# Memory attention of a decoder layer on Trainium2: which weight rests are made by adding transfers, and where the query weight sums are loaded

## The chip, the core and the metric

The kernel runs on one core of a Trainium2 chip. The core has a matrix engine (PE, with PEld for its weight loads), a vector engine (DVE), a scalar engine (ACT), GpSimd (POOL) and SyncE (SP). Each works through its own instructions in order and waits for the others by semaphores. Transfers between DRAM and the on-chip memory are issued by an engine and carried out by 16 DMA engines, which the queues of all issuers share; here SP issues the plain loads and POOL the loads that add onto what is already in the tile ("adding transfers").

The metric is the time of one execution in device microseconds (us), as the median of several runs.

## The reference

One decoder layer over 512 tokens of width 1024 with a memory of 256 rows: a half-step of a gated feed-forward network, token mixing, cross-attention to the memory, a second half-step and a final norm. The change touches the cross-attention alone:

```python
def memory_xattn(h, m, w_xq, w_xkv, w_xo):
    B, S, _ = h.shape
    q = (h @ w_xq).reshape(B, S, XATTN_HEADS, XATTN_HEAD_DIM) * XATTN_HEAD_DIM ** -0.5
    k, v = jnp.split(m @ w_xkv, 2, axis=-1)
    k = k.reshape(B, -1, XATTN_HEADS, XATTN_HEAD_DIM)
    v = v.reshape(B, -1, XATTN_HEADS, XATTN_HEAD_DIM)
    p = jax.nn.softmax(jnp.einsum('bshd,bmhd->bhsm', q, k).astype(jnp.float32), axis=-1)
    o = jnp.einsum('bhsm,bmhd->bshd', p.astype(v.dtype), v)
    return o.reshape(B, S, D_MODEL) @ w_xo
...
        x = x + memory_xattn(rms_norm(x, norm_xattn[l]), rms_norm(mem, norm_mem[l]), w_xq[l], w_xkv[l], w_xo[l])
```

B is 1, S is 512, D_MODEL is 1024, and there are 4 heads of 256.

## The kernel before

Every matrix product is made from operands that are split in two: a head `h` in the type fp32r, and a rest `l`, which is the float32 value minus the head. A product then takes three matmuls: h with h, h with l, l with h. There are two ways to the rest of a weight:

- `split` (L113): ACT copies the raw weight into `h`, DVE subtracts `h` from the raw weight.
- `added` (L1478): ACT copies the raw weight into `h`, ACT writes the negated copy into `l`, and POOL issues a transfer that reads the same weight from DRAM once more and adds it onto `l`.

The **memory stage** (from L1443) computes keys and values of the memory. Its 16 weights `kv`, numbered i = 0 to 15, are 128 x 1024 each (512 KB): i = 0 to 7 are the key weights `in_w_xk`, each with 24 matmuls of 256 columns, and i = 8 to 15 are the value weights `in_w_xv`, each with 12 matmuls of 512 columns. Value weights 8 to 11 add up into the bank `ps_s`, 12 to 15 into `ps_t`. All 16 pass through a ring of three raw tiles (`wr`); `fetch` (L1467) loads the next one on SP's queue. `cut` (L1484) makes head and rest of a weight: into two pairs of half tiles, named `w`, for the weights in `LOOSE`; else into a whole pair, named `wh`/`wl` for i = 5 and 6 and `xqh`/`xql` for the others. `share` (L1473) takes `added` for the weights in `SHARED` and `split` for the rest. Each cut is followed by the fetch of the weight three further on.

From the loop over i on, the order of the instructions on every engine is the order in which the code is written (`ordered`). One turn of the loop: cut one weight ahead (two in the first turn), the matmuls of weight i, the keys of weight i - 1 taken out of their bank, the extras of that turn, and one or two pieces of `work`, which scale the input x and split its sums for the query products (the tiles `K`, `nh`, `nl`). After the last cut the raw tiles serve the query weights of the heads (`load_r`, L1541).

The **query products** of a head (`heads`, L1703) follow a scheme of seven products instead of eight, so they need sums of the query weight `in_w_xq`. The tile `xs` (called `s` in the code, 128 x 1536) holds them: two blocks are loaded by `load_q` (L1529, SP) and completed by an adding transfer in `add_q` (L1535, POOL); the third is a sum of the second with a part of the raw tile `r1`. For head 0 the loop also splits these: `w1` is the pair made from `r1` (its left half is read by the first of the products), `w2` the pair made from `xs`. `part` is `split` for one half of 512 columns. The second product reads the right half of `w2` (the first loaded block), the third the left half (the sum), the fourth the right half of `w1`; the second loaded block is split inside `heads` for a later product.

The extras that the loop places are (NKV is 16):

```python
                if i in (0, 2):
                    load_q(i // 2)
                elif i in (3, 5):
                    add_q(i // 5)
```

Of the kernel before, what the change touches and what calls it, by code (L numbers as in the profile page):

```python
# [71 lines left out]
def hybrid_layer(ctx: ExitStack, tc: tile.TileContext, a: dict):  # L72
# [16 lines left out]
    @contextmanager  # L89
    def ordered():  # L90
        Engine.pinned = True
        yield
        Engine.pinned = False
# [19 lines left out]
    def split(h, l, src):  # L113
        A.activation(h, src, AF.Copy)  # L114
        V.tensor_sub(l, src, f32(h))  # L115

    def wpair():
        return (g.tile([P, 1024], F32R, tag="wh", name="wh", bufs=2),
                g.tile([P, 1024], F32R, tag="wl", name="wl", bufs=2))
# [811 lines left out]
    with tc.tile_pool(name="mix", bufs=1, reuse_waits="tile") as mp:  # L931
# [121 lines left out]
        for c in range(4):  # L1053
            h, l = wload(a["vcat"][:, c * 2 * VC:(c + 1) * 2 * VC], 2 * VC)
            for kk in range(2):
                k = 2 * c + kk
                w = slice(kk * VC, (kk + 1) * VC)
# [385 lines left out]
    with tc.tile_pool(name="xa", bufs=1, reuse_waits="tile") as xp:  # L1443
# [11 lines left out]
        def part(hl, src, j):  # L1455
            split(*hl, src[:, j * 512:j * 512 + 512])
# [4 lines left out]
        kv = [a["w_xk"][m] for m in range(KT)] + [a["w_xv"][f, c] for f in range(2) for c in range(4)]  # L1461
        NKV = len(kv)
        raws, cuts = [], []
        SHARED = (7, 9, 11, 13)
        LOOSE = (0, 1, 2, 7, 8, 9, 12, 13, 14)

        def fetch():  # L1467
# [5 lines left out]
        def share(i, h, l, c):  # L1473
            if i not in SHARED:
                return split(h, l, raws[i][:, c])
            added(h, l, raws[i][:, c], kv[i][:, c])

        def added(h, l, raw, src):  # L1478

            A.activation(h, raw, AF.Copy)  # L1480
            A.activation(l, raw, AF.Copy, scale=-1.0)
            G.dma_start(l, src, accum_op=ALU.add)

        def cut():  # L1484
            i = len(cuts)
            if i in LOOSE:
                cuts.append([[big(F32R, "w0") for _ in range(2)] for _ in range(2)])
                for j in range(2):
                    share(i, cuts[i][0][j], cuts[i][1][j], slice(j * S, j * S + S))
            else:  # L1490
                cuts.append(wpair() if i in (5, 6) else qpair())
                share(i, *cuts[i], slice(0, 1024))
            fetch()
# [6 lines left out]
        def memory(i):  # L1500
            h, l = cuts[i]
            if i < KT:
                pk[i] = bank("d")
                for k in range(KT):
                    for z, (w, m) in enumerate(((h, gh[k]), (h, gl[k]), (l, gh[k]))):
                        w = w[k // 4][:, k % 4 * P:][:, :P] if i in LOOSE else w[:, k * P:(k + 1) * P]
                        T.matmul(pk[i][:, :MEM], w, m, start=k + z == 0, stop=k == KT - 1 and z == 2)
                return
            c = i % 4
            pk[i] = [bank("st"[i // 4 - 2]) for _ in range(MT)] if c == 0 else pk[i - 1]  # L1510
            for kk in range(2):
                k = 2 * c + kk
                w = slice(kk * 512, kk * 512 + 512)
                for t in range(MT):
                    tk = slice(t * P, (t + 1) * P)
                    for z, (m, ww) in enumerate(((gh, h), (gh, l), (gl, h))):
                        T.matmul(pk[i][t], m[k][:, tk], ww[kk] if i in LOOSE else ww[:, w], start=k + z == 0,
                                 stop=k == KT - 1 and z == 2)

        def evacuate(i):  # L1520
            if i < KT:
                split(kh[i], kl[i], pk[i][:, :MEM])
            elif i % 4 == 3:
                for t in range(MT):
                    split(vh[t][i // 4 - 2], vl[t][i // 4 - 2], pk[i][t])
# [3 lines left out]
        def load_q(hd):  # L1529
            w1 = a["w_xq"][2 * hd + 1]  # L1530
            xw[hd]["s"] = xp.tile([P, 1536], F32, tag="S", name="xs3", bufs=2)
            t = xw[hd]["s"][:, 512:].rearrange("p (j c) -> p j c", j=2)
            SY.dma_start(t, bass.AP(w1.tensor, w1.offset, [[1024, P], [0, 2], [1, 512]]))

        def add_q(hd):  # L1535
            w0 = a["w_xq"][2 * hd]
            t = xw[hd]["s"][:, 512:].rearrange("p (j c) -> p j c", j=2)
            G.dma_start(t, bass.AP(w0.tensor, w0.offset, [[1024, P], [P * 1024 + 512, 2], [1, 512]]),
                        accum_op=ALU.add)

        def load_r(hd):  # L1541
            xw[hd]["r1"] = raw_tile()
            SY.dma_start(xw[hd]["r1"], a["w_xq"][2 * hd])

        def load_r2(hd):
            d = xw[hd]
            d["r2"] = xp.tile([P, 1024], F32, tag="R2", name="r2", bufs=1)
            SY.dma_start(d["r2"][:, :512], a["w_xq"][2 * hd + 1][:, 512:])
# [55 lines left out]
        with ordered():  # L1604
            for i in range(NKV):
                for _ in range(1 if i else 2):
                    if len(cuts) < NKV:
                        cut()
                    elif len(cuts) == NKV and "r1" not in xw[0]:
                        load_r(0)  # L1610
                        load_r2(0)
                        load_r(1)
                        load_r(2)
                memory(i)
                if i == 0:
                    st = n3.sums()
                    n3.r = n3.rstd(st, NT)
                elif i == 1:
                    n3.spread()
                if i:  # L1620
                    evacuate(i - 1)
                if i in (0, 2):
                    load_q(i // 2)
                elif i in (3, 5):
                    add_q(i // 5)
                if i == NKV - 4:
                    d = xw[0]
                    d["w2"], w = wpair(), wpair()
                    d["w1"] = [[t[:, c:c + 512] for t in w] for c in (0, 512)]
                    added(*w, d["r1"], a["w_xq"][0])  # L1630
                    part([t[:, 512:] for t in d["w2"]], d["s"], 1)
                elif i == NKV - 3:
                    V.tensor_add(d["s"][:, :512], d["s"][:, 1024:], d["r1"][:, :512])
                    part([t[:, :512] for t in d["w2"]], d["s"], 0)
                for _ in range(0 if i < 2 else 1 if i < 9 else 2):
                    if work:
                        work.pop(0)()
            while work:
                work.pop(0)()
            evacuate(NKV - 1)  # L1640
# [274 lines left out]
```

## Time and profile before

| | |
|---|---|
| time, median of 3 runs | 1245.64 us (1244.54 to 1246.74) |
| time of the profiled execution | 1245.68 us |
| its span, first to last instruction | 1243.9 us |
| mean granted TensorE clock | 0.997 |
| DMA packets, bytes | 64944, 181.38 MB |
| queue q1 (plain loads) | 132.70 MB, 32.4% of the 16 engines' span |
| queue q0 (POOL's transfers) | 46.63 MB, 18.3% |
| chain that ended last, by engine | PE 92%, DVE 3%, DMA 2% |

The time of an execution is a little longer than the span between its first and last instruction (here 1.8 us). The chain that ended last is followed back from the last instruction, at each step to what released it. Of the page's 40 slices, each 31.1 us long, the memory stage fills most of the 24th and the 25th, which read (busy shares in tenths, and GB/s):

| | slice 24 | slice 25 |
|---|---|---|
| PE busy | 9 | 7 |
| DMA busy | 7 | 7 |
| GB/s | 230 | 202 |

### The profile page before, as it was taken

The numbers are of one execution on the slowest core, as the hardware profiler recorded it, in microseconds if no ns is written. First come the engines' busy times: TensorE is split into PE (matmuls) and PEld (weight loads), VectorE is DVE, ScalarE is ACT, GpSimd is POOL, SyncE is SP. The second block draws the span as 40 slices with busy tenths as digits, with TensorE's granted clock in tenths as the row PEclk, the third lists the DMA queues.
The fourth block names the chain that finished last, engine by engine and source line by source line (L and its number), as shares of the span: only waits on it lengthen the run. The fifth ranks groups of instructions, "written<-read, shape, count | busy, mean of one in ns | idle before, by whom it ended". The sixth has DMA issues, their size and how long they took to land.

```text
span 1243.9 us, 19322 instructions
## 1 busy us (share of the span) xinstructions
PE 1226.9 (99%) x7113; PEld 1070.2 (86%) x7113; DVE 992.9 (80%) x2018; ACT 754.0 (61%) x1506; POOL 97.3 (8%) x123
## 2 busy tenths in 40 slices
PE   9999999999999999999999997999999999999997
PEld 7888888879989788888887896997888888888997
DVE  5899888888787978787778667775698888889774
ACT  5466666556555777776874456664456666655553
POOL 0001110221110000000001011000001111100000
PEclk9999999999999999999999999999999999999999
DMA  6737775688544522222234377332456777727441
GB/s 223 186 109 194 187 190 149 188 254 246 138 150 129 168 67 84 81 67 77 68 102 169 102 230 202 102 94 68 111 152 169 188 184 196 178 87 207 134 134 69
DMA packets 64944, 181.38 MB, mean 146 GB/s; under 512 B 6616, under 2 KB 6896, under 8 KB 64848
## 3 DMA queue, kind: packets, MB, share of 16 engines
q1 hardware_dynamic: 45920, 132.70, 32.4%
q0 software_dynamic: 18496, 46.63, 18.3%
q8 instruction: 56, 0.92, 0.3%
q10 hardware_dynamic: 432, 0.81, 0.2%
q14 instruction: 40, 0.33, 0.1%
HBM read 175.87 MB, written 10.07 MB: 149 GB/s over the span
## 4 chain that ended last, share of the span: by engine, by line
PE 92%; DVE 3%; DMA 2%; ACT 1%; issue 1%; DVEq 0%; SPq 0%; POOL 0%; ACTq 0%; POOLq 0%
PE ps_d L139 30%; PE ps_d L87 21%; PE ps_t L87 13%; PE ps_s L87 7%; PE ps_o L87 6%; PE ps_d L1313 4%; PE ps_d L614 2%; PE ps_t L1198 1%; PE ps_s L1111 1%; PE ps_o L1106 1%; PE ps_s L1110 1%; PE ps_o L1105 1%; DMA xql<-in_w_xv_dram 1%; DMA xs<-in_w_xq_dram 1%; PE ps_d L1061 1%
## 5 line engine op out<-in xcount | busy, mean ns | idle before, releaser
L114 ACT ACTIVATE wh<-wr 128x512 fp32r<-128x512 f32 (+2 forms) x158 | 105.0, 695 | 100.7 <-issue 44.6
L139 PE MATMUL ps_d<-xh,wl 128*128 128x512 f32 x360 | 144.6, 402 | 0.1
L139 PE MATMUL ps_d<-xh,wh 128*128 128x512 f32 x360 | 143.3, 398 | 0.0
L139 PE MATMUL ps_d<-xl,wh 128*128 128x512 f32 x360 | 143.2, 398 | 0.0
L115 DVE TENSOR_TENSOR wl<-wr,wh 128x512 fp32r<-128x512 f32 (+2 forms) x158 | 119.0, 775 | 22.7 <-ACT wh L114 20.7
L87 DVE TENSOR_TENSOR wl<-wr,wh 128x1024 fp32r<-128x1024 f32 (+2 forms) x73 | 76.9, 1058 | 25.9 <-ACT wh L87 25.7
L139 PEld LDWEIGHTS ps_d<-xh,wl 128*128 128x128 f32 x360 | 67.8, 188 | 13.8 <-DVE wl L115 0.5
L139 PEld LDWEIGHTS ps_d<-xl,wh 128*128 128x128 f32 x360 | 67.8, 188 | 13.1
L87 ACT ACTIVATE wh<-wr 128x1024 fp32r<-128x1024 f32 (+2 forms) x74 | 67.9, 923 | 18.3 <-PE ps_o L87 4.6
L139 PEld LDWEIGHTS ps_d<-xh,wh 128*128 128x128 f32 x360 | 67.9, 189 | 12.9
L87 PE MATMUL ps_d<-b,wh 128*128 128x512 f32 (+1 forms) x220 | 64.0, 350 | 0.0
L87 DVE TENSOR_TENSOR s<-s,wr 128x512 f32<-128x512 f32 (+1 forms) x84 | 63.9, 760 | 0.0
L87 DVE TENSOR_TENSOR h2l<-s,h2h 128x512 fp32r<-128x512 f32 x68 | 44.1, 688 | 8.4 <-ACT h2h L87 8.1
L87 PE MATMUL ps_o<-t,h2h 128*128 128x256 f32 x272 | 50.4, 283 | 0.0
L87 PE MATMUL ps_d<-n,h2h 128*128 128x512 f32 x136 | 49.9, 401 | 0.1
L87 PE MATMUL ps_d<-b,wl 128*128 128x256 f32 x178 | 49.9, 280 | 0.0
L87 PE MATMUL ps_d<-t,h4h 128*128 128x512 f32 x136 | 49.6, 399 | 0.0
L87 PE MATMUL ps_t<-b,h5h 128*128 128x512 f32 x136 | 49.4, 397 | 0.0
L87 PE MATMUL ps_t<-n,h3h 128*128 128x512 f32 x136 | 49.3, 395 | 0.0
L87 PE MATMUL ps_s<-b,wh 128*128 128x512 f32 x136 | 49.1, 395 | 0.0
L1093 ACT ACTIVATE pth<-ps_t 128x512 fp32r<-128x512 f32 (+1 forms) x64 | 32.6, 524 | 18.7 <-PE ps_t L1198 15.5
L87 ACT ACTIVATE h2h<-s 128x512 fp32r<-128x512 f32 x68 | 39.1, 623 | 7.6 <-DVE s L87 7.6
(567 smaller groups left out, 3906.5 us busy)
## 6 DMA issues: line engine op xcount, KB each, us to landing
wr<-in_w_in_dram SPq DMA_DIRECT2D x29, 512.0 KB, 3.6
wr<-in_w_gate_dram SPq DMA_DIRECT2D x25, 512.0 KB, 5.1
wr<-in_w_up_dram SPq DMA_DIRECT2D x25, 512.0 KB, 5.3
wr<-in_w_down_dram SPq DMA_DIRECT2D x24, 448.0 KB, 3.5
s<-in_w_gate_dram SPq DMA_DIRECT2D x17, 512.0 KB, 4.5
s<-in_w_gate_dram POOLq DMA_DIRECT2D x17, 512.0 KB, 6.0
s<-in_w_up_dram SPq DMA_DIRECT2D x17, 512.0 KB, 4.3
s<-in_w_up_dram POOLq DMA_DIRECT2D x17, 512.0 KB, 6.4
```

The lines of the kernel that those rows point to most:

```text
L87: return lambda *args, **kw: tc.keep_in_program_order(call(*args, **kw))
L114: A.activation(h, src, AF.Copy)
L115: V.tensor_sub(l, src, f32(h))
L139: yield T.matmul(out, w[:, c], m, start=i == 0, stop=i == total - 1)
L614: T.matmul(two[m], w[:, cc], v, start=f == 0 and z == 0, stop=f == NA - 1 and z == 2)
L1061: T.matmul(pv[i][:, :VC], m[k][:, tk], ww[:, w], start=k == 0 and z == 0, stop=k == KT - 1 and z == 2)
L1093: A.activation(h[:, :n], pt[:, :n], AF.Copy)
L1105: T.matmul(po[:, cols], w, h[:, src], start=start, stop=False, skip_group_check=True)
L1106: T.matmul(po[:, cols], w, l[:, src], start=False, stop=False, skip_group_check=True)
L1110: first = T.matmul(out, q[:, tk], kk[0][:, ks], start=True, stop=False)
L1111: T.matmul(out, q[:, tk], kk[1][:, ks], start=False, stop=True)
L1313: yield T.matmul(pj, w[:, c], m, start=n == 0, stop=n == 11)
```

## The change

Three things change. The set of weights whose rest is made by an adding transfer is now 5, 8 and 11 instead of 7, 9, 11 and 13. The raw loads and the additions of the query weight sums of heads 0 and 1 come in later turns of the loop: loads in turns 6 and 12 instead of 0 and 2, additions in turns 8 and 14 instead of 3 and 5. And the rest of head 0's `w1` is no longer made by an adding transfer; it is split in two halves, the left one in turn 12 as before, the right one in turn 14.

```diff
@@ -1461,7 +1461,7 @@
-        SHARED = (7, 9, 11, 13)
+        SHARED = (5, 8, 11)
         LOOSE = (0, 1, 2, 7, 8, 9, 12, 13, 14)
@@ -1619,16 +1619,18 @@
-                if i in (0, 2):
-                    load_q(i // 2)
-                elif i in (3, 5):
-                    add_q(i // 5)
+                if i in (6, 12):
+                    load_q(i // 12)
+                elif i in (8, 14):
+                    add_q(i // 14)
                 if i == NKV - 4:
                     d = xw[0]
                     d["w2"], w = wpair(), wpair()
                     d["w1"] = [[t[:, c:c + 512] for t in w] for c in (0, 512)]
-                    added(*w, d["r1"], a["w_xq"][0])
+                    part(d["w1"][0], d["r1"], 0)
                     part([t[:, 512:] for t in d["w2"]], d["s"], 1)
+                elif i == NKV - 2:
+                    part(d["w1"][1], d["r1"], 1)
                 elif i == NKV - 3:
```

Before, POOL's adding transfers of the memory stage stand in this order (the pairs `w` of `in_w_xk` are weight 7; of `in_w_xv` the pairs `w` are weights 9 and then 13, `xql` is weight 11; `xs` are the query sums of heads 0 and 1, `wl` of `in_w_xq` is the rest of head 0's `w1`):

```order
L87 DMA w_8156<-in_w_xk_dram 128x512
L87 DMA w_8157<-in_w_xk_dram 128x512
L87 DMA xs_8073<-in_w_xq_dram 128x2x512
L87 DMA w_8246<-in_w_xv_dram 128x512
L87 DMA w_8247<-in_w_xv_dram 128x512
L87 DMA xs_8148<-in_w_xq_dram 128x2x512
L87 DMA xql<-in_w_xv_dram 128x1024
L87 DMA w_8400<-in_w_xv_dram 128x512
L87 DMA w_8401<-in_w_xv_dram 128x512
L87 DMA wl<-in_w_xq_dram 128x1024
```

In the changed kernel the same place on POOL reads (`wl` of `in_w_xk` is weight 5, the pair `w` weight 8, `xql` weight 11):

```order
L87 DMA wl<-in_w_xk_dram 128x1024
L87 DMA w_8199<-in_w_xv_dram 128x512
L87 DMA w_8200<-in_w_xv_dram 128x512
L87 DMA xql<-in_w_xv_dram 128x1024
L87 DMA xs_8314<-in_w_xq_dram 128x2x512
L87 DMA xs_8510<-in_w_xq_dram 128x2x512
```

Ten transfers of the stage have become six, and both query sums now stand behind weight 11 instead of ahead of it.

On SP, the plain loads from the first query sum of before (right behind the key weights) to the second one of after; `wr` are raw weights and `r` the right half of a query weight (`load_r2`), and the number behind x counts equal rows:

```order
-L87 DMA xs_8073<-in_w_xq_dram 128x2x512
+L87 DMA wr<-in_w_xv_dram 128x1024 x6
+L87 DMA xs_8314<-in_w_xq_dram 128x2x512
 L87 DMA wr<-in_w_xv_dram 128x1024 x2
-L87 DMA xs_8148<-in_w_xq_dram 128x2x512
-L87 DMA wr<-in_w_xv_dram 128x1024 x6
 L87 DMA wr<-in_w_xq_dram 128x1024
-L87 DMA r_8492<-in_w_xq_dram 128x512
+L87 DMA r_8486<-in_w_xq_dram 128x512
 L87 DMA wr<-in_w_xq_dram 128x1024 x2
-L87 DMA r_8650<-in_w_xq_dram 128x512
+L87 DMA xs_8510<-in_w_xq_dram 128x2x512
```

The first load of a query sum has moved from ahead of all eight value weights to behind six of them, the second from behind two of them to behind the raw query weights.

On ACT, the head copies for the first query products in turns 12 to 14 (`nh` belongs to the split of the input's sums):

```order
-L87 ACTIVATE wh<-wr 128x1024
-L87 ACTIVATE wl<-wr 128x1024
-L87 ACTIVATE wh<-xs_8073 128x512
+L87 ACTIVATE wh<-wr 128x512
+L87 ACTIVATE wh<-xs_8314 128x512
 L87 ACTIVATE nh<-xpl 128x512 x2
-L87 ACTIVATE wh<-xs_8073 128x512
+L87 ACTIVATE wh<-xs_8314 128x512
 L87 ACTIVATE nh<-w3l 128x512
-L87 ACTIVATE nh<-xph 128x512 x4
+L87 ACTIVATE nh<-xph 128x512
+L87 ACTIVATE wh<-wr 128x512
```

Two whole copies have become one half copy here and another half copy further on, and the copies from the query sum stand where they stood.

## The prediction

> **What bounds the kernel now.** First the page, for the engine that sets the end.
>
> ```profile
> span 1243.9 us, 19322 instructions
> PE 1226.9 (99%) x7113; PEld 1070.2 (86%) x7113; DVE 992.9 (80%) x2018; ACT 754.0 (61%) x1506; POOL 97.3 (8%) x123
> ```
>
> PE is busy 1226.9 of 1243.9 us, so only some 17 us of the span can go without removing matmuls. The change removes none. It can gain only where PE stands still or runs slowly, so next comes the table of windows over the stage that it touches (columns: length, then busy time of PE, PEld, DVE, ACT, POOL, then granted clock, DMA share, GB/s).
>
> ```profile
> 720.00:730.00 10.00, 10.00 (x81) 9.73 (x80) 5.79 (x11) 4.67 (x8) 0.00 (x0) 1.00 0.52 165
> 721.30:745.90 24.60, 24.60 (x209) 24.60 (x208) 15.68 (x29) 14.58 (x27) 5.88 (x6) 1.00 0.80 227
> 745.90:765.75 19.85, 13.49 (x51) 9.94 (x50) 16.16 (x33) 11.36 (x20) 2.60 (x3) 0.91 1.06 286
> 765.75:776.74 10.99, 10.99 (x49) 9.01 (x48) 7.23 (x12) 7.78 (x13) 0.84 (x1) 1.00 0.34 68
> 776.74:800.00 23.26, 23.26 (x198) 23.25 (x197) 16.07 (x31) 13.90 (x32) 1.20 (x1) 1.00 0.34 83
> ```
>
> The eight key weights run in 721.3 to 745.9 without an idle moment. The first four value weights (i = 8 to 11) take 19.85 us with PE busy for 13.49 of them, at a granted clock of 0.91; the last four (12 to 15), 48 matmuls as well, take 10.99. The DMA share is 1.06 in the slow window, that is, all 16 engines are full. What PE waits for there, by the waits and the timeline of PE:
>
> ```profile
> PE ps_s L87 <- DMA xql<-in_w_xv_dram: 3.7, 1, 3.7
> PE ps_s L87 <- DMA w<-in_w_xv_dram: 2.6, 2, 1.7
> ...
> 750.71 0.50 PE L87 MATMUL ps_s<-w,gh 128*128 128x512 f32 x1 [1.66 <-DMA w<-in_w_xv_dram]
> 753.32 0.50 PE L87 MATMUL ps_s<-w,gh 128*128 128x512 f32 x1 [0.95 <-DMA w<-in_w_xv_dram]
> 761.52 0.50 PE L87 MATMUL ps_s<-xql,gh 128*128 128x512 f32 x1 [3.74 <-DMA xql<-in_w_xv_dram]
> ```
>
> All three wait for adding transfers from POOL's queue: the two halves of the rest of weight 9 and the rest of weight 11. The chain of waits tells why the last was late:
>
> ```profile
> 732.50 9.04 DMA xs<-in_w_xq_dram
> ...
> 749.29 12.19 DMA xql<-in_w_xv_dram
> 761.52 4.38 PE ps_s L87 x11
> 765.91 11.00 PE ps_t L87 x48
> 776.91 1.43 PE ps_d L87 x12
> ```
>
> A query-weight load, then the adding transfer of weight 11 with 12.19 us to landing. The PE rows also price a matmul: 11.00 us for 48 is 0.229 each, 4.38 for 11 is 0.398, so after the long wait PE was slow; a query product takes 1.43. The issues in 712 to 800 and the two queues there (88 us):
>
> ```profile
> q1 hardware_dynamic: 3779, 11.62, 39.2%
> q0 software_dynamic: 1968, 4.20, 26.6%
> ...
> xs<-in_w_xq_dram POOLq DMA_DIRECT2D x3, 512.0 KB, 14.8
> w<-in_w_xv_dram POOLq DMA_DIRECT2D x4, 256.0 KB, 10.6
> xql<-in_w_xv_dram POOLq DMA_DIRECT2D x1, 512.0 KB, 12.2
> wl<-in_w_xq_dram POOLq DMA_DIRECT2D x1, 512.0 KB, 5.3
> ...
> 732.80 0.88 POOL L87 DMA_DIRECT2D w<-in_w_xk_dram  x1 [71.93 <-ACT w L87]
> 769.80 0.84 POOL L87 DMA_DIRECT2D wl<-in_w_xq_dram  x1 [12.98 <-PE ps_t L87]
> ```
>
> q1 (plain loads) took 0.392 x 88 = 34.5 us of all engines for 11.62 MB, so a 512 KB load costs 34.5 x 0.524 / 11.62 = 1.56 us; q0 (adding) 0.266 x 88 = 23.4 us for 4.20 MB, so 512 KB cost 2.92. An adding transfer is nearly two loads. POOL's first and last add of the stage are the last two rows. An add lands after 5.3 us in a quiet stretch (wl, at 769.8) and after 10.6 to 14.8 in a full one.
>
> **The change part by part.** *The limit of the gain.* Equal work takes 19.85 us in one half and 10.99 in the other: 8.86 us, of which 1.66 + 0.95 + 3.74 = 6.35 are idle and the other 2.5 are slow and restarting matmuls (11 x (0.398 - 0.229) = 1.9 in the one row alone). Every other window around shows PE full, so 8.86 is also the most that can be won.
>
> [...]
>
> *What DMA loses and what is moved.* Adding transfers in the stage go from weights 7, 9, 11, 13 and the query weight to 5, 8, 11: two fewer, 2 x 2.92 = 5.8 us of the engines. The two query loads and their two adds (2 x 1.56 + 2 x 2.92 = 9.0 us) leave the places behind weights 7 and 9. Ahead of weight 11's add POOL had, from 732.8, weight 7, a query add, weight 9, a query add: 4 x 2.92 = 11.7 us, and 2.9 for itself. With the plain loads of weights 8 to 14 and the two query loads (9 x 1.56 = 14.0) that is 28.6 us of full engines between 728.8 and 761.5: the queue explains the delay. Now, until weight 11 is wanted, there are the adds of 5, 8, 11 (8.8), loads 8 to 13 and one query load (7 x 1.56 = 10.9): 19.7 us of engine time. If nothing stalls, weight i is wanted at 745.91 + (i - 8) x 12 x 0.229, weight 11 at 754.2 and its rest 0.2 later. From 728.5 that is 25.9 us for 19.7: 6 us spare.
>
> *The three adds that stay*, each from its activation to its matmul:
>
> ```profile
> 726.48 1.04 ACT L87 ACTIVATE wh<-wr 128x1024 fp32r<-128x1024 f32 x1
> 729.01 0.60 ACT L87 ACTIVATE rb<-ps_t 128x512 f32<-128x512 f32 x1 [1.50 <-PE ps_t L87]
> ...
> 737.61 0.28 PE L87 MATMUL ps_d<-gh,wl 128*128 128x256 f32 x1
> 745.91 0.63 PE L87 MATMUL ps_s<-w,gh 128*128 128x512 f32 x2
> ```
>
> Weight 5: ACT makes wh at 726.48 and now also the negated copy, 1.0 us, in the 1.50 us that it spent idle before rb, so at no cost. POOL issues at about 728.6; landing lies between 733.9 (5.3, quiet) and 740.8 (12.2, full), wanted at 737.61: a wait of 0 to 3.2 us. The window 720 to 730 has a DMA share of 0.52 and loses the query load, so it is nearer to the quiet row: 0. Weight 8: the raw weight landed at 734.4 behind a query load that now goes (1.56), and four activations take 2.2 us:
>
> ```profile
> 734.38 1.15 ACT L87 ACTIVATE w<-wr 128x512 fp32r<-128x512 f32 x2 [0.27 <-DMA wr<-in_w_xv_dram]
> 738.06 2.19 ACT L87 ACTIVATE w<-wr 128x512 fp32r<-128x512 f32 x4 [1.74 <-DMA wr<-in_w_xv_dram]
> ```
>
> So its halves are issued near 734 and 736 and wanted at 746.1 and 747.5. By 10.6 us they land at 744.6 and 746.6; quiet, sooner; with 2 us more, a wait of about 1: I take 0. Weight 11: ACT did it at 747 because its raw weight came late:
>
> ```profile
> 744.22 1.06 ACT L87 ACTIVATE xqh<-wr 128x1024 fp32r<-128x1024 f32 x1 [3.70 <-DMA wr<-in_w_xv_dram]
> 746.99 1.06 ACT L87 ACTIVATE xqh<-wr 128x1024 fp32r<-128x1024 f32 x1 [1.13 <-DMA wr<-in_w_xv_dram]
> ```
>
> These waits of ACT for raw weights come from the same full engines. With them gone ACT follows PE, one weight behind, and reaches weight 11 near 742 to 744.5; POOL issues at 744 to 746.5. Landing: 749.3 to 758.7 against 754.4, so a wait of 0 to 4.3. The spare 6 us speaks for the lower part: 0. The spread of the three is what keeps a queue from forming.
>
> *Work that goes from DMA to DVE.* Weights 7, 9, 13 and the query weight are now subtracted on DVE, weights 5 and 8 no longer:
>
> ```profile
> 757.75 1.29 DVE L87 TENSOR_TENSOR w<-wr,w 128x512 fp32r<-128x512 f32 x2
> 740.56 0.42 DVE L87 TENSOR_TENSOR kl<-ps_d,kh 128x256 fp32r<-128x256 f32 x1 [2.36 <-ACT kh L87]
> 745.31 1.23 DVE L87 TENSOR_TENSOR xql<-wr,xqh 128x1024 fp32r<-128x1024 f32 x1 [3.01 <-ACT xqh L87]
> 756.01 0.42 DVE L87 TENSOR_TENSOR K<-yt,K 128x256 fp32r<-128x256 f32 x1 [1.97 <-ACT K L87]
> 773.39 2.49 DVE L87 TENSOR_TENSOR nl<-xph,nh 128x512 fp32r<-128x512 f32 x4
> ```
>
> Four pairs of 1.29 come, one pair and one whole tile (1.23) go: +2.6 us, +3.9 after 732 (the whole tile was earlier). What hides it: DVE was busy 31.80 of 44.74 us from 732 to 776.74.
>
> ```profile
> 732.00:776.74 44.74, 38.38 (x215) 32.85 (x215) 31.80 (x61) 27.30 (x50) 9.32 (x10) 0.96 0.87 229
> ```
>
> Its last rests for the query products end at 773.39 + 2.49 = 775.9, and the first product that reads them starts three products (3 x 1.43) after 776.74, at 781.0: 5.1 us in hand. DVE must absorb 8.86 (less time) + 3.9 (more work) - 5.1 = 7.7 us of its 12.9 idle; the three long gaps quoted are 7.3 of these and all stem from late raw weights, and short ones make up the rest. It fits, tightly: 0, at worst some 4.
>
> *The query sums.* The first sum is loaded near 743 and added near 748, behind weight 11 on POOL. ACT reads it after the fourth value weight's copies, near 759. By the 5.3 and 14.8 rows (plus POOL's own order) it lands at 753 to 763. ACT is in order: its copy and nine more (0.55 each by the row of four), the two value copies (0.6) and the copy that the third product needs (0.4) are 7.1 us of work, and that product starts at 767.9 + 2 x 1.43 = 770.8. So a landing up to 763.7 costs nothing. The second sum is added near 765 and read by DVE after 775: nothing. SP's loads of weights 14 and 15 now stand behind the first query load, 1.56 us later on engines with room: nothing.
>
> The sum: 1245.68 (the profiled execution; its span 1243.9 with 1.8 around it; 0.04 from the median 1245.64) - 8.86 + 0.2 for a stray wait at weight 8 = **1237.0 us**.
>
> **The rivals.** *One add is still late.* Weight 5 (up to 3.2) or weight 11 (up to 4.3) keeps a wait, about 1238 to 1241.3, and to 1243.2 where a wait as long as the 3.74 brings 1.9 us of slow matmuls again. For it: 12.19 us for a whole tile is what this trace has under load. Against it: the load is what is taken away.
>
> *VectorE becomes the bound.* If its gaps do not close, up to 4 us of the gain are lost: 1238 to 1241. For it: 3.9 us more work in 8.9 us less. Against: its gaps have their cause in the transfers.
>
> *The wait only moves.* If the engines stay as full as now, the rest of weight 11 lands at 761.5 again and PE waits there for all that was won elsewhere: 1244 to 1246, no change. For it: three of the five adds stay ahead of 762 and the loads are the same. Against: 19.7 us of transfers where there were 28.6.
>
> *ACT hangs on the first query sum* and the kernel is slower. The sum is asked for in program order by ACT, so everything behind it waits. From a landing at 763.7 each us costs one; the gain of 8.9 is used up at 772.6, and at 775.5 the time is 1248.6. That needs 27 us from the issue near 748; the longest median here is 14.8. That the edit does not do what it says I leave out: the order in which the queues stand shows the adds gone and the loads moved.
>
> **How the numbers follow.** Forecast, all waits gone (1236.8 to 1238): 0.72. One add still late: 0.15. VectorE: 0.05. The wait moves: 0.04. ACT on the query sum: 0.04, a quarter of it within 0.2%. With 1 us for the spread of the runs (1244.54 to 1246.74) the range is 1235.6 to 1241.3, which takes in nearly all of the first three. Within 0.2% (2.5 us, about what a measurement of this kernel can tell from no change) is 1243.1 to 1248.1. Faster 0.92, same 0.05, slower 0.03.
>
> **What would show it.** Right: no PE idle in the value weights, some 22 us from the first of them to the query products, granted clock 1.00, DMA share clearly under 1 until weight 11's add, which lands in 6 to 10 us; ACT with no long wait for a raw value weight. Wrong: a wait of PE for wl (weight 5) near 737.6, for w (weight 8) near 746 or xql near 754; a wait of ACT for xs with PE idle at the third query product; DVE without gaps and PE waiting for its rests. The forecast fails most easily if adding transfers take 12 us even on half-empty engines, since then weights 5 and 11 are both late.

## The result and the profile after

| | before | after |
|---|---|---|
| time, median | 1245.87 us (1244.54 to 1246.74, 4 runs) | 1237.88 us (1236.66 to 1238.88, 4 runs) |
| ratio, 95% interval | | 0.9936 [0.9919, 0.9954] |
| profiled execution | 1245.68 us | 1236.66 us |
| predicted | | 1237.0 us, range 1235.6 to 1241.3 |

The change saves 8.0 us of the medians and 9.0 us between the two profiled executions. The page of the changed kernel begins:

```profile
span 1234.9 us, 19316 instructions
PE 1225.7 (99%) x7113; PEld 1069.0 (87%) x7113; DVE 994.3 (81%) x2023; ACT 751.5 (61%) x1503; POOL 93.9 (8%) x119
```

PE's busy time fell by 1.2 us (1226.9 before) and the span by 9.0, so 7.8 us of what went is time in which PE stood still. The windows, with the same columns and mostly the same bounds as before:

```profile
721.30:745.90 24.60, 24.60 (x209) 24.55 (x208) 18.30 (x36) 15.92 (x28) 2.59 (x3) 1.00 0.76 213
728.50:754.30 25.80, 25.80 (x186) 24.31 (x185) 20.68 (x41) 16.45 (x33) 4.62 (x5) 1.00 0.96 255
745.90:765.75 19.85, 19.85 (x88) 16.03 (x87) 18.28 (x34) 11.36 (x22) 2.03 (x2) 1.00 0.92 265
765.75:776.74 10.99, 10.99 (x82) 10.36 (x82) 9.14 (x16) 8.48 (x17) 1.18 (x1) 1.00 0.31 50
```

PE is busy for every moment of all four, the clock is 1.00, and the query products begin at 768.36 where they began at 776.74 (rows of PE's timelines). The waits of PE over the whole execution hold no transfer any more:

```profile
PE ps_t L87 <- DVE warm L87: 1.0, 1, 1.0
PE ps_d L87 <- ACT xh L87: 0.3, 1, 0.3
PE ps_s L987 <- ACT wh L114: 0.2, 1, 0.2
```

The adding transfers of the three memory weights landed like this (issues of 712 to 800: size, median us to landing), and the third only just in time, as the timeline of the weight loads and matmuls shows:

```profile
wl<-in_w_xk_dram POOLq DMA_DIRECT2D x1, 512.0 KB, 7.2
w<-in_w_xv_dram POOLq DMA_DIRECT2D x2, 256.0 KB, 7.6
xql<-in_w_xv_dram POOLq DMA_DIRECT2D x1, 512.0 KB, 8.0
...
746.66 0.84 POOL L87 DMA_DIRECT2D xql<-in_w_xv_dram  x1 [7.36 <-ACT kh L87]
754.70 0.19 PEld L87 LDWEIGHTS ps_s<-xql,gh 128*128 128x128 f32 x1 [0.42 <-DMA xql<-in_w_xv_dram]
754.70 0.50 PE L87 MATMUL ps_s<-xql,gh 128*128 128x512 f32 x1
```

### The profile page after: what moved, and what is told of

It is laid out like the page before. It is cut to its first block, busy times and chain, and to the rows that moved or that the text cites. A ratio compares the mean times of both kernels' runs of the same rounds, so it can differ in the third digit from the quotient of the medians.

```text
span 1234.9 us, 19316 instructions
## 1 busy us (share of the span) xinstructions
PE 1225.7 (99%) x7113; PEld 1069.0 (87%) x7113; DVE 994.3 (81%) x2023; ACT 751.5 (61%) x1503; POOL 93.9 (8%) x119
## 4 chain that ended last, share of the span: by engine, by line
PE 95%; DVE 3%; ACT 1%; DMA 1%; issue 0%; DVEq 0%; SPq 0%; ACTq 0%
PE ps_d L139 31%; PE ps_d L87 22%; PE ps_t L87 13%; PE ps_s L87 8%; PE ps_o L87 6%; PE ps_d L1313 4%; PE ps_d L614 2%; PE ps_t L1198 1%; PE ps_s L1111 1%; PE ps_o L1106 1%; PE ps_s L1110 1%; PE ps_o L1105 1%; PE ps_d L1061 1%; DVE F L971 1%; PE ps_t L1278 0%; PE ps_s L987 0%
## 5 line engine op out<-in xcount | busy, mean ns | idle before, releaser
L87 PEld LDWEIGHTS ps_d<-b,wh 128*128 128x128 f32 x220 | 38.6, 188 | 6.0
```

Source lines behind the costliest of these rows:

```text
L87: return lambda *args, **kw: tc.keep_in_program_order(call(*args, **kw))
```

## The experiments

The first four runs take the change apart. Only the sums moved:

```diff
         SHARED = (7, 9, 11, 13)
-                if i in (0, 2):
-                    load_q(i // 2)
-                elif i in (3, 5):
-                    add_q(i // 5)
+                if i in (6, 12):
+                    load_q(i // 12)
+                elif i in (8, 14):
+                    add_q(i // 14)
```

> Only the query sums are moved (loads to turns 6 and 12, additions to turns 8 and 14); the adding transfers stay at weights 7, 9, 11, 13 and the query weight. Theory (engine time ahead of weight 11 decides): the two sums' loads and adds, 9.0 us of full engines, leave the place ahead of weight 11, so PE waits for neither weight 9 nor weight 11; but weight 13's adds now stand behind weight 11's and the first sum's on POOL, two adds of 2.92 us on top of the loads, so PE waits 2 to 5 us for the halves of weight 13 in the ps_t bank. Time 1239 to 1243 us. Rival (the choice of the weights and their spacing is what counts): the waits for weights 9 and 11 stay, 1245 us. Rival (only the sums count): no wait at all, 1237 to 1238.

1240.91 us, ratio 0.9957 [0.9941, 0.9973]: as the theory had it. PE's waits, from the timeline of this kernel:

```profile
754.77 0.51 PE L87 MATMUL ps_s<-xql,gh 128*128 128x512 f32 x1 [0.26 <-DMA xql<-in_w_xv_dram]
762.60 0.50 PE L87 MATMUL ps_t<-w,gh 128*128 128x512 f32 x1 [2.02 <-DMA w<-in_w_xv_dram]
764.90 0.50 PE L87 MATMUL ps_t<-w,gh 128*128 128x512 f32 x1 [0.65 <-DMA w<-in_w_xv_dram]
```

The waits for weight 9 are gone and that for weight 11 is down to 0.26; the wait has moved on to weight 13 (`ps_t`), whose adds stand behind weight 11's and the first sum's. Weight 11's add was issued at 746.40 (749.29 before) and landed in 8.3 us (12.2 before).

Only the set of weights:

```diff
-        SHARED = (7, 9, 11, 13)
+        SHARED = (5, 8, 11)
```

> Only the set of weights with adding transfers is changed to 5, 8, 11; the query sums are loaded and added where they were before, and the query weight's rest is made by an adding transfer. Theory (engine time): ahead of weight 11's add stand the adds of 5 and 8 and both sums, as much as before, with two sum loads; the engines stay full, PE waits for weight 8's halves by 0 to 2 us and for weight 11 by 3 to 5 us: 1241 to 1245 us. Rival (number and spacing of the weights' adds is what counts): no wait, 1237 to 1238.

1240.55 us, ratio 0.9957 [0.9945, 0.9969], a little below the expected 1241 to 1245. PE waits a little for each of the three (the totals of its waits):

```profile
PE ps_s L87 <- DMA xql<-in_w_xv_dram: 1.1, 1, 1.1
PE ps_d L87 <- DMA wl<-in_w_xk_dram: 1.0, 1, 1.0
PE ps_s L87 <- DMA w<-in_w_xv_dram: 0.6, 1, 0.6
```

The theory had 3 to 5 us for weight 11, because by its count as much engine time stands ahead of that add as before. The wait was 1.1. The add was issued 1.0 us later than before (750.32 for 749.29), yet it landed in 8.3 us and not 12.2. Ahead of it, weight 5's add was issued at 729.29, where weight 7's had been issued at 732.80. So it counted here when transfers were issued, and not only how many there were; whether the missing adds of weight 13 had a part was not tried by itself.

Each half of the change alone gives about 5 us of the 8. Both shorten the same wait for weight 11 (3.74 us before, 0.26 and 1.1 here), so their gains do not add up.

The changed kernel with the query weight's rest made by an adding transfer again:

```diff
-                    part(d["w1"][0], d["r1"], 0)
+                    added(*w, d["r1"], a["w_xq"][0])
                     part([t[:, 512:] for t in d["w2"]], d["s"], 1)
-                elif i == NKV - 2:
-                    part(d["w1"][1], d["r1"], 1)
```

> The changed kernel, but the rest of head 0's w1 is again made by an adding transfer, as before. Theory: that transfer is issued near 762, when the loads thin out, and its 2.92 us of engines lie behind everything that PE waited for; w1 is read at 768.4 by the first product. With 5.3 us to landing (the quiet row of before) there is 1 us in hand, with 8 us PE waits 2 us at the first query product: 1237.5 to 1240. Rival (every adding transfer taken away counts, wherever it stands): 1 us or more slower through the value weights, with waits there.

1239.07 us, ratio 0.9943 [0.9922, 0.9963]; the four runs are 1237.23, 1237.63, 1240.50 and 1240.59. The profiled one (1237.63) has no wait at the first query product. It has one of 0.76 us for weight 8's adding transfer, at 748.48, which the query weight's own transfer, issued only at 763.46, cannot have caused. This part of the change is worth nothing that these runs could tell; where the two higher runs lose 3 us was not seen.

The changed kernel with the same number of adds, but next to each other:

```diff
-        SHARED = (5, 8, 11)
+        SHARED = (9, 10, 11)
```

> The changed kernel with the three adding transfers packed at weights 9, 10, 11 instead of spread over 5, 8, 11: the same count, the same bytes, the same query sums. Theory (engine time ahead of the due time): the three adds cannot start before raw weight 9 has landed near 738, so 8.8 us of adds and the loads of 12 to 14 and the sum fall on the 16 us up to weight 11's due time of 754.3; PE waits 2 to 4 us, for weight 11 or for 10 and 11 together: 1239 to 1242. Rival (only the count of adds matters): no wait, 1237 to 1238.

1239.27 us, ratio 0.9946 [0.9930, 0.9961]. The time is the expected one, its reason is not. The adds of weights 10 and 11 landed in some 10.7 and 10.1 us (their median is 10.4), where weight 11's took 8.0 in the changed kernel, but PE waited only 0.24 us for weight 11 and not at all for 9 and 10. It waited at the third query product, for ACT. The timeline of ACT leads back from there:

```profile
757.10 1.15 ACT L87 ACTIVATE w<-wr 128x512 fp32r<-128x512 f32 x2 [3.43 <-DMA wr<-in_w_xv_dram]
...
768.76 0.63 ACT L87 ACTIVATE wh<-xs 128x512 fp32r<-128x512 f32 x1 [3.47 <-DVE xs L87]
...
773.38 0.37 ACT L87 ACTIVATE ps_d<-ps_d 128x256 f32<-128x256 f32 x1
...
773.80 0.50 PE L87 MATMUL ps_d<-K,wh 128*128 128x256 f32 x2 [1.27 <-ACT ps_d L87]
```

A raw value weight came late (3.43 us of ACT's time), so DVE came late to the sum of the query weight, ACT waited for that sum, and behind it in order stands the copy of `ps_d` without which the third product cannot start. Packing the adds made little of a queue that PE felt; what PE felt came by the late raw weight.

The next four ran together. The changed kernel once more as what to compare with:

> The changed kernel once more, beside the next three on the same chip, as what they are compared with. Both theories: 1236.5 to 1239 us; the profile shows whether the landing of weight 11's adding transfer exactly when it is wanted (PE's weight load waited 0.4 us for it) was chance.

1237.66 us (five runs: 1236.84, 1236.88, 1237.66, 1240.31, 1240.87), ratio 0.9946 [0.9932, 0.9960]. In its profile the weight loads waited 0.3 us for weight 8 and 0.2 for weight 11: just in time again, so the close landing was not chance.

No adding transfer for any memory weight:

```diff
-        SHARED = (5, 8, 11)
+        SHARED = ()
```

> The changed kernel without any adding transfer for a memory weight: the rests of 5, 8 and 11 are subtracted on DVE too. Theory: DMA loses 3 x 2.92 us, ACT three negated copies (3.2 us), DVE gets 1.23 + 1.29 + 1.23 = 3.75 us. In the changed kernel DVE has no gap from 748.5 to 766, and the rest that the third query product needs at 771.2 is ready at 767.3, so 3.9 us are in hand and raw weights come sooner: no wait beyond 1 us, 1237 to 1239. Rival (VectorE is the bound without adding transfers): the query products wait 2 to 4 us for DVE's rests, 1239.5 to 1242.

1235.79 us (all five runs between 1235.74 and 1236.58), ratio 0.9922 [0.9910, 0.9935]. This beats both kernels: every run lies below the lowest of the changed kernel beside it (1236.84), though the two intervals against the kernel before still touch. The chain that `packed` showed, here in the changed kernel (DVE's sum, ACT's wait for it, ACT's copy of `ps_d`, the third product):

```profile
765.26 0.68 DVE L87 TENSOR_TENSOR xs<-xs,wr 128x512 f32<-128x512 f32 x1
765.98 0.63 ACT L87 ACTIVATE wh<-xs 128x512 fp32r<-128x512 f32 x1 [3.47 <-DVE xs L87]
770.60 0.38 ACT L87 ACTIVATE ps_d<-ps_d 128x256 f32<-128x256 f32 x1
771.23 0.40 PE L87 MATMUL ps_d<-K,wh 128*128 128x256 f32 x2
```

and in the kernel without adds:

```profile
763.77 0.68 DVE L87 TENSOR_TENSOR xs<-xs,wr 128x512 f32<-128x512 f32 x1
764.49 0.63 ACT L87 ACTIVATE wh<-xs 128x512 fp32r<-128x512 f32 x1 [3.32 <-DVE xs L87]
769.30 0.37 ACT L87 ACTIVATE ps_d<-ps_d 128x256 f32<-128x256 f32 x1
770.54 0.40 PE L87 MATMUL ps_d<-K,wh 128*128 128x256 f32 x2
```

With adds the copy ends at 770.98, 0.25 us before PE needs it; without them at 769.67, 0.87 us before. DVE has three more rests to make (3.75 us) and is still 1.49 us earlier at the sum: it works without a wait from 730.55 up to the sum, while in the changed kernel it waits for ACT's heads up to 748.52. ACT waits less for raw value weights (0.75, 0.46 and 1.22 us, for 2.29, 2.04 and 0.69) and has three negated copies fewer to make; which of the two counts for more was not tried.

The first query sum as late as it can be:

```diff
-                if i in (6, 12):
-                    load_q(i // 12)
-                elif i in (8, 14):
-                    add_q(i // 14)
+                if i in (12, 13):
+                    load_q(i - 12)
+                if i in (12, 14):
+                    add_q(i // 14)
```

> The changed kernel with the first query sum loaded and added in turn 12, right ahead of its use, and the second loaded in turn 13. The load then stands behind the raw query weights on SP, near 761, and the sum is complete near 772. Theory of the prediction's fourth rival: ACT waits in order for the sum, everything behind it is late, and from a landing at 763.7 each us costs one: 8 us and more, 1245 to 1248, slower than the changed kernel and about the time of before, with the wait at the second and third query product. Rival (slack behind the sum hides most of it): under 4 us, 1238 to 1241.

1248.46 us, ratio 1.0018 [1.0009, 1.0027]: slower than before. Timeline of ACT and PE:

```profile
771.89 0.63 ACT L87 ACTIVATE wh<-xs 128x512 fp32r<-128x512 f32 x1 [11.71 <-DMA xs<-in_w_xq_dram]
...
772.57 0.50 PE L87 MATMUL ps_o<-K,wh 128*128 128x256 f32 x2 [2.96 <-ACT wh L87]
...
780.12 0.80 PE L87 MATMUL ps_d<-K,wh 128*128 128x256 f32 x2 [5.22 <-ACT ps_d L87]
```

The sum was there at 771.89 and the third product started at 780.12: 8.2 us of ACT's list behind the sum, where the prediction had counted 7.1. That product started at 771.02 in the kernel beside it, so 9.1 us are lost, and by an estimate some 2 more by slow matmuls behind the wait: 20 of them started in 4.44 us (780.12 to 784.56) at a clock of 0.50, where 12 of a query product take 1.43 us at 1.00.

More plain loads:

```diff
+                elif i in (3, 5):
+                    extra = xp.tile([P, 1536], F32, tag="S", name="extra", bufs=2)
+                    SY.dma_start(extra[:, :1024], a["w_xq"][i])
+                    SY.dma_start(extra[:, 1024:], a["w_xq"][i + 1][:, :512])
```

> The changed kernel with two more plain loads of 768 KB each, into tiles that nothing reads, on SP in turns 3 and 5, ahead of weights 12 and 14; POOL's queue is as it was. 2 x 2.34 = 4.7 us of engine time more ahead of weight 11. Theory as the prediction put it (6 us of engine time spare up to weight 11): no wait over 0.5 us, 1237 to 1239. Rival (the engines are as good as full up to weight 11, share 0.96, and its add lands just when it is wanted, so nothing is spare): PE waits 3 to 5 us for weight 11 or for the raw weights behind it, 1240.5 to 1243.

1238.49 us, ratio 0.9943 [0.9930, 0.9957], 0.8 us above the changed kernel beside it: the time that the first theory gave, but with a longer wait for weight 11 than its 0.5 us. PE waited twice; the last two lines are ACT and POOL ahead of the first wait:

```profile
755.91 0.50 PE L87 MATMUL ps_s<-xql,gh 128*128 128x512 f32 x1 [0.96 <-DMA xql<-in_w_xv_dram]
773.33 0.50 PE L87 MATMUL ps_d<-K,wh 128*128 128x256 f32 x2 [0.72 <-ACT ps_d L87]
...
745.45 1.06 ACT L87 ACTIVATE xqh<-wr 128x1024 fp32r<-128x1024 f32 x1 [2.92 <-DMA wr<-in_w_xv_dram]
747.75 0.84 POOL L87 DMA_DIRECT2D xql<-in_w_xv_dram  x1 [8.25 <-ACT kh L87]
```

Of 4.7 us more in front of weight 11, PE felt 0.96 there, and not because the add was slower: it landed in 8.1 us (8.0 in the changed kernel), but its raw weight came late (ACT waited 2.92 us for it, where it had waited 2.04) and so it was issued 1.1 us later (747.75 for 746.66). By the difference of 4.7 and 0.96, an estimate, the engines had some 3.7 us of work that could wait, at a DMA share of 0.96 without the loads and 1.00 with them (728.5 to 754.3): the loads of weights further on.

The last four ran together. The kernel before with the one edit to its set:

```diff
-        SHARED = (7, 9, 11, 13)
+        SHARED = ()
```

> The kernel before with one edit: no memory weight has an adding transfer any more; the query sums stay in turns 0 to 5 and the query weight keeps its adding transfer. Theory: PE waited only for weights' adding transfers, so with all of them gone the place of the sums (9.0 us of engine time ahead of weight 11) no longer matters; raw weights are loaded in time (18.4 us of transfers in the 26 us up to weight 11), DVE follows as in the kernel without adds: 1236 to 1238 us, no wait in the value weights. Rival (the early sums are a cost of their own, by the raw weights that they delay): PE waits 1 to 4 us for rests that DVE makes late, 1238 to 1241.

1236.93 us (1236.21 to 1237.38), ratio 0.9927 [0.9913, 0.9941]. The early sums cost nothing that these runs can tell once no weight waits for an add. What PE waited for is the query weight's rest, which this kernel still adds:

```profile
769.48 0.39 PE L87 MATMUL ps_d<-K,wl 128*128 128x256 f32 x1 [0.86 <-DMA wl<-in_w_xq_dram]
```

Which of the three adds makes the changed kernel's runs spread:

```diff
-        SHARED = (5, 8, 11)
+        SHARED = (5, 11)
```

> The changed kernel with adding transfers for weights 5 and 11 alone; weight 8 is split on DVE. The changed kernel's runs lie at 1237 and, in some, at 1239 to 1241, those without adds all within 1 us of 1236. Theory (weight 8's halves come just in time, a wait of 0.8 us in one profile, and make the spread): all runs within 1 us, at 1236 to 1237. Rival (weight 11 makes it, its add landed when it was wanted): runs at 1236.5 and some at 1239 to 1241 again.

```diff
-        SHARED = (5, 8, 11)
+        SHARED = (8,)
```

> The changed kernel with an adding transfer for weight 8 alone. Theory (weight 8 makes the spread): runs at 1236.5 and some at 1239 to 1241. Rival (weight 11, or the three together): all runs within 1 us, at 1236 to 1237.

1237.18 us (1236.74 to 1237.33), ratio 0.9931 [0.9918, 0.9944], and 1236.61 us (1235.92 to 1236.89), ratio 0.9927 [0.9914, 0.9940]. All ten runs are close together, so neither weight 8 alone nor 5 and 11 made a spread here, though five runs each are few: of the changed kernel and `w1_added`, which have all three, 4 of 13 runs were above 1240. Those 4 stand among runs near 1237. That they tip over the 0.25 us of the chain above would fit, but no profiled execution was such a run, so it stays open.

More work for DVE, in the kernel without adds:

```diff
+                if 2 <= i < 8:
+                    extra = xp.tile([P, 1536], F32, tag="S", name="extra", bufs=2)
+                    V.tensor_sub(extra[:, :512], x[i], x[i - 1])
+                    V.tensor_sub(extra[:, 512:1024], x[i], x[i - 2])
```

> The kernel without adding transfers for weights, with twelve more subtractions of 128 x 512 on DVE, two in each of turns 2 to 7, into a tile that nothing reads: 12 x 0.605 = 7.3 us of DVE. Theory (without adds DVE has about 5 us in hand up to the third query product: its rest is ready at 765.8 and wanted near 770.8): PE waits 2 to 3 us, for the rests of value weights 12 to 15 and of the query weights, 1238 to 1239.5. Rival (DVE is the bound already): all 7.3 us are lost, 1243. Rival (DVE has more room than that): under 1 us lost, below 1237.

1244.55 us, ratio 0.9983 [0.9973, 0.9994], 8.8 us above the kernel without adds (by the ratios to the kernel before, which each set of runs has beside it: 0.9983 and 0.9922, so some 7.6 us). The rival that VectorE is as good as the bound holds. The timeline of PE:

```profile
741.30 0.39 PE L87 MATMUL ps_d<-gh,wh 128*128 128x256 f32 x1 [0.72 <-DVE kl L87]
744.64 0.39 PE L87 MATMUL ps_d<-gh,w 128*128 128x256 f32 x1 [0.24 <-DVE kl L87]
777.28 0.80 PE L87 MATMUL ps_d<-K,wh 128*128 128x256 f32 x2 [4.53 <-ACT ps_d L87]
```

Of 7.3 us more, 5.5 came out as waits of PE, so DVE had some 1.8 us in hand, not 5. Of the rest of the loss some 1.4 us are, by an estimate, slow matmuls behind the longest wait: 13 of them started in 2.94 us (777.28 to 780.22) at a clock of 0.50, where 12 take 1.43 us at 1.00.

## Why the prediction was right, and where its reasons were not

**The limit and the sum held.** The value weights were worth 8.86 us by the difference of their two halves; from the first of them to the query products it is now 22.3 us (746.05 to 768.36) and was 30.8 (745.91 to 776.74), 8.5 us less; the profiled execution was 9.0 us shorter and the median 8.0. PE's clock shows that the slow matmuls went with the waits: 1.00 in every window, where it was 0.91 in the slow one of before. That the sum came out so closely is luck in part: two of its terms came out at 0 only just, with a weight load that waited 0.42 us and a copy that had 0.25 us to spare (below).

**That late adding transfers were the cause is shown** from both sides: taking the sums away from ahead of weight 11 gives about 5 us (`sums_only`), and with no weight waiting for an add the sums may stay where they were, for a gain no smaller than the change's (`no_adds_old_sums`, ratio 0.9927 for 0.9936). Weight 11's rest was there 6.8 us sooner (754.7 for 761.5), 2.6 of it because its add was issued sooner and 4.2 because it landed faster. The prediction's measure of the cause, engine time ahead of the add, is too coarse: in `set_only` it was as much as before, and the wait fell from 3.74 to 1.1.

**The three adds: the values were right, one of them by nothing to spare.** Landing took 7.2, 7.6 and 8.0 us, between the quiet 5.3 and the full 12.2. For weight 11 the step "The spare 6 us speaks for the lower part: 0" was mis-sized: its weight load waited 0.42 us, the DMA share up to there was 0.96 and not clearly under 1, and 4.7 us more of loads cost a wait of 0.96. From 728.5 to 754.3 the engines had 0.96 x 25.8 = 24.8 us of work where the prediction had counted 19.7. It had left out what SP issued there for later: weights 14 and 15, the last at about 750, and the first query weights at 752.70 and 753.26. Some of that could wait, so about 3.7 us were spare and not 6.

**"The spread of the three is what keeps a queue from forming" was worth little.** Packed at 9, 10 and 11, the later two took 2 to 3 us longer to land, but they cost PE 0.24 us; the rest of the 1.4 us that `packed` lost came by a late raw weight.

**DVE: the term was 0 as predicted, but its reason was wrong.** The prediction had 5.1 us in hand between DVE's last rests and the fourth product, the first to read them. But the third product comes first, and what it needs last is ACT's copy of `ps_d`, in order behind DVE's sum of the query weight; in the changed kernel this leaves 0.25 us (0.18 in `after_again`). The rival "VectorE becomes the bound" was given 0.05 and came within a quarter of a microsecond. `more_dve`, `packed` and `more_loads` all fail at just that place. Nor did ACT's waits for raw value weights vanish, as was expected of a right forecast; 2.29, 2.04 and 0.69 us of them remain.

**The query sums: right.** Loaded at 744.24 and added at 750.93, the first was there when ACT read it at 760.84. `late_sum` bears out the rival's mechanism, and a time slower than before, at a higher price than it gave. For a sum read at 771.89 one for one from 763.7 is 8.2 us; the third product moved by 9.1, since ACT's list is 8.2 us and not 7.1, and the slow matmuls behind the wait, which the price left out, make it 10.8 (1248.46 for 1237.66).

**The query weight's own adding transfer** had no price of its own beside its 2.92 us of the engines, and `w1_added` shows none clear of the spread of its runs.

## What to carry to other kernels

An adding transfer relieves the vector engine at the price of DMA time: here three of them spared it 3.75 us, and each cost, by the estimate from the queues' shares, 2.92 us of all 16 engines, nearly two loads of 1.56. Before, that fell in a stretch where the engines were full (DMA share 1.10 from 740 to 750) and the vector engine itself waited for late raw weights (3.01 us for a head, for whose raw weight ACT had waited 3.70), and the changed kernel without any for the memory weights was faster than with its three (1235.79 us for 1237.66). When a wait goes, follow every in-order queue up to the next consumer and not just the tile that it reads: the margin, 0.25 us in the changed kernel, lay in a copy that stood behind the sum, not in the sum. Full DMA engines are no proof that a transfer is late: in `more_loads` their share was 1.00 from 728.5 to 754.3, and weight 11's add landed in 8.1 us, where it took 8.0 at 0.96. Look for the one whose landing a waiting engine names.

## What the runs showed of the hardware

In the kernel before, the granted clock fell 0.72 us after the end of PE's pause of 3.74 us, when PE was already at work again. PE stood from 757.78 to 761.52, and the windows (same columns as above) give:

```profile
757.78:761.52 3.74, 0.00 (x1) 0.00 (x0) 3.74 (x9) 2.05 (x4) 0.00 (x0) 1.00 1.08 296
761.52:762.24 0.72, 0.72 (x3) 0.62 (x4) 0.69 (x3) 0.70 (x2) 0.00 (x0) 1.00 1.07 259
762.24:765.66 3.42, 3.42 (x10) 2.63 (x9) 2.53 (x4) 0.60 (x1) 0.00 (x0) 0.50 0.99 325
```

In `late_sum` it fell 1.87 us after a pause of 2.97 us, shorter than the 3.74 of before, and read 0.50 through the 5.22 us wait that followed:

```profile
769.60:772.57 2.97, 0.01 (x2) 0.00 (x1) 0.02 (x1) 0.68 (x2) 0.00 (x0) 1.00 1.12 201
772.57:774.44 1.87, 1.65 (x11) 1.44 (x12) 1.87 (x4) 0.99 (x2) 0.00 (x0) 1.00 0.72 129
774.44:780.12 5.68, 0.46 (x3) 0.17 (x2) 4.98 (x10) 5.04 (x11) 0.00 (x0) 0.50 0.01 1
780.12:784.68 4.56, 4.56 (x21) 4.56 (x22) 2.56 (x5) 2.20 (x4) 0.00 (x0) 0.50 0.00 0
```

The waits of 1.66 and 0.95 us in the kernel before left it at 1.00 (749.05 to 757.78), and so did the 2.02 us of `sums_only` (759 to 768). In `more_dve` the pause was longer, 4.53 us, and the clock fell at 776.90, before PE started again at 777.28:

```profile
772.75:776.90 4.15, 0.00 (x0) 0.00 (x0) 4.00 (x7) 4.15 (x10) 0.80 (x1) 1.00 0.67 102
776.90:780.32 3.42, 3.04 (x14) 3.05 (x15) 2.71 (x5) 1.33 (x5) 0.00 (x0) 0.50 0.17 30
```

Counted from the start of the pause, the clock fell after 4.46 us in the kernel before, 4.84 in `late_sum` and 4.15 in `more_dve`. The stretch at half clock lasted 3.42 us in the kernel before and in `more_dve`, and 10.24 us in `late_sum`. What sets these lengths no run shows.
